# Sums kept in HBM, a gate applied in the last block, seven raw buffers and sums of weights by adding transfers, in the MLP of a two-layer trunk

## The chip, the cores and the metric

The kernel runs on one core of a Trainium2 chip. The metric is the device time of one execution in microseconds (us); the median of three runs is 2183.13 us (2182.64 to 2187.89). Engines are named as in the profile: PE multiplies matrices, PEld loads its weights, DVE (vector), ACT (scalar) and POOL work on tiles, and SP only issues transfers.

## The reference

Two layers over 256 tokens of width 2048. Each has an attention part and an MLP, both modulated by vectors computed from a condition `c`. In short:

```python
cond = silu(c)
for l in range(2):
    mod = cond @ w_ada[l] + b_ada[l]                # 2048 x 12288
    sh_a, sc_a, g_a, sh_m, sc_m, g_m = split(mod, 6)
    h = rmsnorm(x) * (1 + sc_a) + sh_a
    mix = attention(h, w_in[l], ...)                 # two kinds of heads
    x = x + g_a * (mix @ w_o[l])
    h = rmsnorm(x) * (1 + sc_m) + sh_m
    y = square(relu(h @ w_mlp_in[l])) @ w_mlp_out[l] # 2048 -> 8192 -> 2048
    x = x + g_m * y
return rmsnorm(x, final_norm_g)
```

Everything is float32.

## The kernel before

**Weights.** Each float32 product is made of three: a weight of 128 rows by 2048 columns (1 MB) is loaded by SP into a buffer with the tag `raw`, ACT copies its high part `hi` (line 152, in halves of 1024 columns), DVE subtracts to get the low part `lo` (line 155), and PE multiplies high by high, high by low and low by high. There are five `raw` buffers and four each of `hi` and `lo`. Loads are issued in the order of SP's queue, and one waits until a buffer is free.

**Conditioning loads.** `w_ada` is 192 such loads of 1 MB. They use the same five buffers. They are not multiplied on PE: DVE multiplies each by `cond` and sums it in one instruction (line 381), writing to `macc`, and then makes columns of `mod`. When they are loaded is set by a rate: each call of `weights` adds `self.rate` to a credit, and for each whole unit one load is issued (`more_ada`). `RATE_S` is the rate in the paired part of a block, `RATE_R` in its second part, and the other `RATE_` names hold in other stages.

**The MLP.** Its 8192 hidden columns are cut into four blocks of 2048 (`fb` 0 to 3). A block first makes the hidden activations and then multiplies them with `w_mlp_out`. Layer 0's first block goes through `first_block`; all others go through `block_by_seven`, which works in pairs of 128 hidden columns: two `wides` (a weight each, 32 matmuls, to bank `ps`) make the pair's hidden tile; then `seven` multiplies it with the left 1024 output columns by seven products of 2x2 blocks in place of eight. The products go in two steps, `five` and `two`, into seven PSUM banks `pp`, which are summed over the pairs of the block. The weights of that step are one load (`raw<-in_w_ms`) and three sums of its parts, which DVE writes to a second `raw` buffer under the name `comb` (lines 1223 to 1225). Line 1223 is the largest, 128 x 1024. There are eight pairs in a block, five in the first block of layer 1, whose first three pairs are made another way (`plain`).

After the pairs comes the second part of the block, called its tail below: the right 1024 columns as two groups (`c` = 2 and 3), each with four weights (`in_w_m`) and 96 matmuls into two banks `pr`.

**What is kept.** The seven sums of a block are added to tiles `acc` in SBUF: by ACT's copy to `part` and a transfer of POOL that adds 256 KB (`acc<-part`, lines 1145 and 1146), or by DVE in the last block (line 1142). The right columns of each block are multiplied by the gate `self.row` (named `bias` in the profile; DVE, line 1151) and added to the residual `x` by a transfer of POOL (`x<-yg`, line 1154). The gate of a layer is computed in its second block.

**Order.** The program is written stage by stage, and a tile scheduler sets the order of instructions on each engine. Each engine and each queue runs in its order.

Of the kernel before, what the change touches and what calls it, by code (L numbers as in the profile page):

```python
# [97 lines left out]
RATE_A0, RATE_V, RATE_A1, RATE_A2, RATE_K, RATE_K1, RATE_M0, RATE_R = 1.1, 1.6, 0.7, 1.2, 0.6, 0.4, 1.0, 1.25  # L98
RATE_S = 0.0, 0.3
# [3 lines left out]
class Trunk:  # L103
    def __init__(self, ctx, tc, io):
# [4 lines left out]
        self.up = pool("up", 44)  # L109
        self.tp = pool("tp", 8)  # L110
# [58 lines left out]
    def raw(self, src, width):  # L169
        raw = self.wp.tile([P, width], F32, tag="raw", name=self.name("raw"), bufs=5)  # L170
        self.nc.sync.dma_start(raw, src)
        return raw
# [189 lines left out]
    def ada_load(self):  # L362
        w = self.wp.tile([P, D], F32, tag="raw", name=self.name("ada"), bufs=5)
# [519 lines left out]
    def layer(self, l, acc=None):  # L883
# [164 lines left out]
        acc, late = ({}, []) if l else self.first_block(h, banks)  # L1048
        for fb in range(1 - l, NFB):
            self.block_by_seven(l, fb, h, banks if l and fb == 0 else [], acc, late)  # L1050
        self.quiet = False

    def first_block(self, h, banks):

        io = self.io
        hid, acc, late = [], {}, []
# [3 lines left out]
        for m in range(12, NK, 2):  # L1060
            ps = self.wides([io["w_m10"][m + j - 12] for j in range(2)], h)
            hid += self.relu2(self.joined(ps, self.t("sum")))
        for c in range(4):
            pss = self.rows(io["w_m2"][0, 0], hid, c)
            if c == 0:
                acc[2], acc[4] = [self.copy(ps, "acc") for ps in pss]
            elif c == 1:
                acc[3], acc[7] = [self.copy(ps, "acc") for ps in pss]
                self.nc.vector.tensor_tensor(acc[4], acc[7], acc[4], ALU.subtract)
            else:  # L1070
                late += [(self.copy(ps, "y"), t, c) for t, ps in enumerate(pss)]
        return acc, late

    def block_by_seven(self, l, fb, h, banks, acc, late):

        io = self.io
        hid, steps, sums = [], [], []
        plain = len(banks)
        self.rate = RATE_S[l] if fb == 0 or not l else 0.0
        for m in range(0, plain, 2):  # L1080
            hid += self.relu2(self.joined(banks[m : m + 2], self.t("sum")))
        for m in range(plain, NK, 2):
            both = self.t("sum")
            for j in range(2):
# [3 lines left out]
                if m > plain + 2:  # L1088
                    steps.pop(0)()
# [3 lines left out]
            steps += self.seven(io[f"w_ms{l}"][fb, m // 2], parts, r, sums, m == plain, m == NK - 2)  # L1093
            if fb == 1 and m == 2:
                self.gate(l, 5)
            while m > 4 and late:
                self.add_late(*late.pop(0))
        for f in steps:
            f()
        self.rate = RATE_R  # L1100
        end = fb == NFB - 1
        light = [lambda g=g: self.gather(acc, sums, g, end) for g in ((1, 2), (3, 5), (7, 6), (4,))]
        halves = []
        if end:
            done = self.final if l else lambda pss, c: self.updates(pss, c, True)
            light += [lambda: halves.extend(self.merged(acc))]
            light += [lambda c=c: done(halves[c], c) for c in range(2)]
        elif fb:
            def done(pss, c):
                for t in range(2):  # L1110
                    self.add_late(pss[t], t, c)
        else:
            def done(pss, c):
                late.extend((self.copy(ps, "y"), t, c) for t, ps in enumerate(pss))
        light.pop(0)()
        pss = [self.bank("pr") for _ in range(2)]
        for kq in range(4):
            self.rows_by_k(pss, self.weights(io["w_m2"][l, fb, 2, kq]), hid, kq)
            if light:
                light.pop(0)()  # L1120
# [3 lines left out]
        if plain:  # L1124
            self.both_by_k([self.weights(io[f"w_ms{l}"][fb, m // 2]) for m in range(0, plain, 2)], hid, acc)
        if end:
            pss = self.rows(io["w_m2"][l, fb], hid, 3, True)
        else:
            pss = [self.bank("pr") for _ in range(2)]
            for kq in range(4):  # L1130
                self.rows_by_k(pss, self.weights(io["w_m2"][l, fb, 3, kq]), hid, kq)
        done(pss, 3)

    def gather(self, acc, sums, group, end):

        flat = lambda v: v.rearrange("p a b -> p (a b)")
        for i in group:
            ps = sums[i - 1]
            if i not in acc:
                acc[i] = self.copy(ps, "acc")  # L1140
            elif end:
                self.nc.vector.tensor_tensor(acc[i], ps, acc[i], ALU.add)
            else:
                t = self.t("part")
                self.nc.scalar.activation(t, ps, AF.Copy)
                self.nc.gpsimd.dma_start(flat(acc[i]), flat(t), accum_op=ALU.add)

    def add_late(self, y, t, c):

        tmp = self.t("yg").rearrange("p a b -> p (a b)")  # L1150
        self.nc.vector.tensor_tensor(
            tmp, y.rearrange("p a b -> p (a b)"), self.row[:, 512 * c : 512 * c + 512], ALU.mult
        )
        self.nc.gpsimd.dma_start(self.xs_of(t, c), tmp, accum_op=ALU.add)
# [521 lines left out]
```

## Time and profile before

| | |
|---|---|
| median of the runs | 2183.13 us |
| the profiled execution | 2184.29 us, of which 2182.5 us are the span of the profile |
| PE busy | 2125.5 us, 97% |
| DVE busy | 1868.8 us, 86% |
| ACT busy | 1268.2 us, 58% |
| POOL busy | 49.7 us, 2% |
| transfers issued by SP, share of 16 DMA engines | 586.41 MB, 72.0% |
| transfers issued by POOL | 18.12 MB, 3.9% |

Busy shares are means over stages, so each stage is to be read by itself. A row of a group of instructions gives line, engine, operation, written and read tiles, count, then busy time and mean duration in ns, then the engine's idle time ahead of it and what ended that. A row of a transfer gives its issuer, count, size and the median time in us from issue to landing. `x` in a row of the windows is a count of instructions. Some matmuls are missing in the records, and a busy PE is not always at its peak.

### The profile page before, as it was taken

How to read it: one execution, taken by the hardware profiler on the slowest of the kernel's cores; microseconds unless marked ns; L12 is line 12 of the kernel's file. 1: busy time of each engine (PE TensorE's matmuls, PEld its weight loads, DVE VectorE, ACT ScalarE, POOL GpSimd, SP SyncE). 2: the span in 40 equal slices, each digit the busy share in tenths (PEclk: the TensorE clock that was granted, in tenths of full speed). 3: DMA queues.
4: the chain of work that ended last, by engine and by line, in shares of the span. 5: the costliest groups of instructions: out<-in, count | busy, mean ns of one | idle time of the engine just before them, and what ended most of it. 6: DMA issues, size and time to landing. Idle time of an engine off the chain costs nothing.

```text
span 2182.5 us, 29752 instructions
## 1 busy us (share of the span) xinstructions
PE 2125.5 (97%) x11339; PEld 1828.8 (84%) x11339; DVE 1868.8 (86%) x2558; ACT 1268.2 (58%) x1872; POOL 49.7 (2%) x67
## 2 busy tenths in 40 slices
PE   7999999999999899899989999999999999999998
PEld 6899887998888788788869998878878888888886
DVE  8889888888899798788998898789997985895898
ACT  6555663554467366456555566536655674774674
POOL 0000000000000000100000000000000010000000
PEclk8999999999999999999999999999999999999999
DMA  9989899789965965976679779896696767468453
GB/s 397 422 335 347 318 360 345 275 313 373 366 211 203 371 230 190 299 280 220 224 262 338 273 289 337 312 347 247 212 344 253 234 226 230 174 219 257 178 195 130
DMA packets 94304, 607.64 MB, mean 278 GB/s; under 512 B 10640, under 2 KB 11088, under 8 KB 27344
## 3 DMA queue, kind: packets, MB, share of 16 engines
q1 hardware_dynamic: 85536, 586.41, 72.0%
q0 software_dynamic: 7904, 18.12, 3.9%
q8 instruction: 89, 1.46, 0.2%
q10 hardware_dynamic: 720, 1.19, 0.1%
q14 instruction: 55, 0.45, 0.1%
HBM read 589.66 MB, written 3.18 MB: 272 GB/s over the span
## 4 chain that ended last, share of the span: by engine, by line
PE 81%; DVE 9%; DMA 6%; ACT 2%; issue 1%; ACTq 0%; DVEq 0%
PE ps L218 18%; PE ps L221 10%; PE pr L312 6%; PE pr L313 6%; PE pr L315 6%; DVE lo L155 4%; DMA raw<-in_w_m 3%; PE pk L261 3%; PE pp L1216 3%; PE pp L1215 3%; PE pp L1214 3%; DVE ada L381 2%; PE pk L195 2%; PE pk L199 2%; PE pk L198 2%; PE pk L285 2%
## 5 line engine op out<-in xcount | busy, mean ns | idle before, releaser
L152 ACT ACTIVATE hi<-raw 128x1024 fp32r<-128x1024 f32 (+2 forms) x714 | 706.1, 1004 | 552.9 <-DMA raw<-in_w_m 143.2
L155 DVE TENSOR_TENSOR lo<-raw,hi 128x1024 fp32r<-128x1024 f32 (+2 forms) x714 | 808.3, 1153 | 211.8 <-ACT hi L152 131.5
L381 DVE SCALAR_TENSOR_TENSOR ada<-ada,cond 128x2048 f32<-128x2048 f32 x192 | 437.2, 2284 | 13.5 <-DMA ada<-in_w_ada 12.8
L218 PE MATMUL ps<-h,hi 128*128 128x512 f32 x1856 | 442.6, 391 | 0.4 <-DVE sum L1382 0.3
L218 PEld LDWEIGHTS ps<-h,hi 128*128 128x128 f32 x1856 | 344.4, 188 | 75.0 <-DVE sum L1382 5.0
L312 PE MATMUL pr<-hi,hidh 128*128 128x512 f32 x576 | 229.4, 398 | 17.5 <-ACT hi L152 17.3
L221 PEld LDWEIGHTS ps<-h,lo 128*128 128x128 f32 x1856 | 237.4, 191 | 8.7
L221 PE MATMUL ps<-h,lo 128*128 128x256 f32 x1856 | 240.1, 283 | 0.0
L313 PE MATMUL pr<-hi,hidl 128*128 128x512 f32 x576 | 227.2, 395 | 0.0
L312 PEld LDWEIGHTS pr<-hi,hidh 128*128 128x128 f32 x576 | 110.0, 191 | 47.8 <-ACT hi L152 25.0
L315 PE MATMUL pr<-lo,hidh 128*128 128x512 f32 x576 | 144.7, 392 | 5.4 <-DVE lo L155 5.4
L155 DVE TENSOR_TENSOR lo<-comb,hi 128x1024 fp32r<-128x1024 f32 x106 | 128.9, 1218 | 7.7 <-PE ps L221 7.2
L315 PEld LDWEIGHTS pr<-lo,hidh 128*128 128x128 f32 x576 | 108.4, 189 | 29.5 <-DVE lo L155 7.1
L313 PEld LDWEIGHTS pr<-hi,hidl 128*128 128x128 f32 x576 | 110.1, 191 | 22.8
L152 ACT ACTIVATE hi<-comb 128x1024 fp32r<-128x1024 f32 x106 | 111.4, 1054 | 24.5 <-PE pp L1216 14.7
L195 PE MATMUL pk<-h,hi 128*128 128x256 f32 x320 | 90.4, 285 | 0.2 <-ACT h L716 0.2
L199 PE MATMUL pk<-h,lo 128*128 128x256 f32 x320 | 90.5, 283 | 0.0
L198 PE MATMUL pk<-h,hi 128*128 128x256 f32 x320 | 90.5, 283 | 0.0
L1381 ACT ACTIVATE sum<-ps 128x256 f32<-128x256 f32 x110 | 42.2, 383 | 80.5 <-PE ps L221 80.5
L261 PE MATMUL pk<-hf,w 128*128 128x256 f32 x384 | 83.9, 379 | 0.0
L1215 PE MATMUL pp<-lo,sh 128*128 128x512 f32 x212 | 83.4, 393 | 0.2 <-DVE lo L155 0.2
L1214 PE MATMUL pp<-hi,sh 128*128 128x512 f32 x212 | 81.9, 394 | 1.0 <-ACT sh L1205 1.0
(295 smaller groups left out, 3521.3 us busy)
## 6 DMA issues: line engine op xcount, KB each, us to landing
ada<-in_w_ada SPq DMA_DIRECT2D x192, 1024.0 KB, 6.9
raw<-in_w_m SPq DMA_DIRECT2D x182, 1024.0 KB, 6.3
raw<-in_w_ms SPq DMA_DIRECT2D x56, 1024.0 KB, 5.2
raw<-in_w_o SPq DMA_DIRECT2D x32, 1024.0 KB, 6.5
raw<-in_w_m SPq DMA_DIRECT2D x24, 768.0 KB, 5.9
raw<-in_w_dv SPq DMA_DIRECT2D x16, 1024.0 KB, 6.1
raw<-in_w_t SPq DMA_DIRECT2D x12, 1024.0 KB, 6.6
w<-in_w_a SPq DMA_DIRECT2D x24, 384.0 KB, 13.5
```

The costliest lines, as they stand in the source:

```text
L152: ins = self.nc.scalar.activation(hi, v, AF.Copy)
L155: ins = self.nc.vector.tensor_tensor(lo, v, hi.bitcast(F32), ALU.subtract)
L198: mm(ps, hi, x[1], start=False, stop=False, skip_group_check=shared)
L218: mm(ps.rearrange("p a b -> p (a b)"), part(w, k, 0), x[2], start=k == 0, stop=False)
L221: mm(ps[:, 0], part(w, k, 1), x[0], start=False, stop=k == nk - 1)
L261: self.nc.tensor.matmul(ps, v, whole[k], start=first, stop=last, skip_group_check=True)
L312: mm(ps, xh[:, c], part(i, 0), start=kq == 0 and i == 0, stop=False)
L313: mm(ps, xl[:, c], part(i, 0), start=False, stop=False)
L315: self.last_mm = mm(ps, xh[:, c], part(i, 1), start=False, stop=kq == 3 and i == 3)
L381: ins = nc.vector.scalar_tensor_tensor(w, w, 1.0, self.cond, ALU.mult, ALU.mult, accum_out=acc[:, i : i + 1])
L1214: nc.tensor.matmul(ps, x[0], wh, start=first, stop=False)
L1215: nc.tensor.matmul(ps, x[0], wl, start=False, stop=False)
```

## The change

It has five parts.

- The seven sums of a block and its right columns are kept in tiles `kept` in HBM. ACT copies each bank to `part`, and a transfer of POOL writes it (the first time) or adds it there (`keep`, `keep_tile`, `keep_left`, `keep_right`). In the last block, `last_right` has POOL load the eleven kept tiles of 256 KB into SBUF, and DVE adds the last sums to them.
- The gate is computed and applied in the last block only: `rows(2)` and `rows(3)` multiply the kept right columns by it, and POOL adds them to `x`.
- Seven buffers `raw` in place of five; the pool `up` (2 KB per partition) goes from 44 to 40, `tp` from 8 to 6, and the scratch for POOL's transfers from 4096 to 2048.
- The largest sum of weights is made by ACT (a copy with scale -1) and a transfer of POOL that adds 512 KB to it, one pair ahead of its use (`sums_of_weights`); DVE still makes it for the last pair of a block. That is 46 by transfer and 7 by DVE, where DVE made 53.
- The rates: conditioning loads are fewer in the tails (`RATE_R`, `RATE_E`) and some are now in the paired part of all blocks of layer 0.

Over the program POOL's rows go from 72 to 168, DVE's from 2274 to 2206, ACT's from 1674 to 1738; PE's and SP's stay at 10616 and 595.

```diff
-RATE_A0, RATE_V, RATE_A1, RATE_A2, RATE_K, RATE_K1, RATE_M0, RATE_R = 1.1, 1.6, 0.7, 1.2, 0.6, 0.4, 1.0, 1.25
-RATE_S = 0.0, 0.3
+RATE_A0, RATE_V, RATE_A1, RATE_A2, RATE_K, RATE_K1, RATE_M0 = 1.1, 1.6, 0.6, 1.1, 0.6, 0.4, 0.9
+RATE_S, RATE_R, RATE_E = (0.45, 0.25), (0.6, 0.4), 0.5
+RAWS = 7
...
-        self.rate = RATE_S[l] if fb == 0 or not l else 0.0
+        self.rate = RATE_S[l]
...
-                if m > plain + 2:
-                    steps.pop(0)()
+                if j == 0 and pairs:
+                    pairs[-1][0]()
+                if len(pairs) > 1:
+                    pairs[-2][1 + j]()
...
+        self.rate = RATE_E if end else RATE_R[l]
         if end:
...
+            return self.last_right(l, hid, sums)
+        light = [lambda g=g: [self.keep(i, sums[i - 1]) for i in g] for g in ((1, 2), (3, 5), (7, 6), (4,))]
         light.pop(0)()
+        for c in (2, 3):
+            pss = [self.bank("pr") for _ in range(2)]
+            for kq in range(4):
+                self.rows_by_k(pss, self.weights(io["w_m2"][l, fb, c, kq]), hid, kq)
+                if light:
+                    light.pop(0)()
+            self.keep_right(pss, c)
...
+    def last_right(self, l, hid, sums):
...
+        def loads():
+            for i in list(range(1, 8)) + [(t, c) for c in (2, 3) for t in range(2)]:
+                acc[i] = self.u("acc")
+                self.nc.gpsimd.dma_start(acc[i].rearrange("p a b -> p (a b)"), self.kept[i])
...
+        def rows(c):
+            for t in range(2):
+                y = acc[t, c].rearrange("p a b -> p (a b)")
+                op(y, y, self.row[:, 512 * c : 512 * c + 512], ALU.mult)
+                self.nc.gpsimd.dma_start(self.xs_of(t, c), y, accum_op=ALU.add)
...
+    def keep_tile(self, i, t):
+        t = t.rearrange("p a b -> p (a b)")
+        if i in self.kept:
+            self.nc.gpsimd.dma_start(self.kept[i], t, accum_op=ALU.add)
         else:
...
+            self.kept[i] = self.dp.tile([P, 2 * T], F32, name=f"kept{self.n}")
+            self.nc.gpsimd.dma_start(self.kept[i], t)
...
+        def sums_of_weights(by_dve=False):
+            raw = self.raw(src, 2048)
+            comb = self.wp.tile([P, 2048], F32, tag="raw", name=self.name("comb"), bufs=RAWS)
+            if by_dve:
+                add(comb[:, :1024], raw[:, 512:1536], raw[:, :1024], ALU.subtract)
+            else:
+                nc.scalar.activation(comb[:, :1024], raw[:, :1024], AF.Copy, scale=-1.0)
+                nc.gpsimd.dma_start(comb[:, :1024], raw[:, 512:1536], accum_op=ALU.add)
+            st["raw"], st["comb"] = raw, comb
...
         def five():
+            raw, comb = st["raw"], st["comb"]
             if first:
                 sums.extend(self.bank("pp") for _ in range(7))
-            raw = self.raw(src, 2048)
-            comb = self.wp.tile([P, 2048], F32, tag="raw", name=self.name("comb"), bufs=5)
-            add(comb[:, :1024], raw[:, 512:1536], raw[:, :1024], ALU.subtract)
             add(comb[:, 1024:1536], raw[:, 1024:1536], comb[:, :512], ALU.subtract)
```

How it moves instructions. First SP's queue, in the tail of the third block of layer 0; `in_w_m` are weights of the right columns, `in_w_ada` conditioning loads. Before:

```order
L171 DMA raw_8153<-in_w_m 128x2048
L365 DMA ada_8166<-in_w_ada 128x2048
L171 DMA raw_8198<-in_w_m 128x2048
L365 DMA ada_8209<-in_w_ada 128x2048
L171 DMA raw_8238<-in_w_m 128x2048
L365 DMA ada_8250<-in_w_ada 128x2048
L171 DMA raw_8284<-in_w_m 128x2048
L365 DMA ada_8295<-in_w_ada 128x2048
L365 DMA ada_8297<-in_w_ada 128x2048
L171 DMA raw_8323<-in_w_m 128x2048
```

The same place now:

```order
L172 DMA raw_8236<-in_w_m 128x2048
L172 DMA raw_8274<-in_w_m 128x2048
L366 DMA ada_8284<-in_w_ada 128x2048
L172 DMA raw_8318<-in_w_m 128x2048
L366 DMA ada_8330<-in_w_ada 128x2048
L172 DMA raw_8356<-in_w_m 128x2048
L172 DMA raw_8391<-in_w_m 128x2048
L366 DMA ada_8401<-in_w_ada 128x2048
L172 DMA raw_8427<-in_w_m 128x2048
L172 DMA raw_8471<-in_w_m 128x2048
```

Between five weights there were five conditioning loads; between seven there are now three.

Second DVE's row in the first pairs of layer 0's fourth block; `ps` are banks of the `wides`, `comb` the sums of weights (and, with 128 columns, those of the hidden tile). Before:

```order
L1206 TENSOR_TENSOR sl_8549<-comb_8543,sh_8548 128x512
L1224 TENSOR_TENSOR comb_8714<-raw_8712,comb_8714 128x512
L155 TENSOR_TENSOR lo_8719<-raw_8712,hi_8718 128x512
L1225 TENSOR_TENSOR comb_8714<-comb_8714,raw_8712 128x512
L155 TENSOR_TENSOR lo_8726<-raw_8712,hi_8725 128x1024
L1382 SCALAR_TENSOR_TENSOR sum_8552<-ps_8598,sum_8552 128x256
L1223 TENSOR_TENSOR comb_8864<-raw_8862 128x1024
```

The same place now:

```order
L382 SCALAR_TENSOR_TENSOR ada_8481,macc_88<-ada_8481,cond 128x2048
L156 TENSOR_TENSOR lo_8584<-raw_8581,hi_8583 128x1024
L156 TENSOR_TENSOR lo_8588<-raw_8581,hi_8587 128x1024
L1415 SCALAR_TENSOR_TENSOR sum_8469<-ps_8470,sum_8469 128x256
L1258 TENSOR_TENSOR comb_8629<-raw_8627,comb_8629 128x512
L1259 TENSOR_TENSOR comb_8629<-comb_8629,raw_8627 128x512
L156 TENSOR_TENSOR lo_8636<-raw_8633,hi_8635 128x1024
L156 TENSOR_TENSOR lo_8640<-raw_8633,hi_8639 128x1024
L1415 SCALAR_TENSOR_TENSOR sum_8469<-ps_8517,sum_8469 128x256
L382 SCALAR_TENSOR_TENSOR ada_8591,macc_88<-ada_8591,cond 128x2048
```

The 128x1024 sum is gone from the row, conditioning rows have come in, and the two remaining sums (lines 1258 and 1259, 1224 and 1225 before) stand further ahead of the low parts made from `comb`. They read what POOL's transfer has added.

Third, where the copy of that chain and those adds stand, in a pair in the middle of a block of layer 1. ACT's row now, `comb_17333` being the sum (before, ACT had no such row):

```order
L153 ACTIVATE hi_17204<-comb_17031 128x1024
L153 ACTIVATE hi_17217<-raw_17215 128x1024
L1231 ACTIVATE sh_17130<-comb_17125 128x512
L1250 ACTIVATE comb_17333<-raw_17331 128x1024
L1414 ACTIVATE sum_17134<-ps_17135 128x256
L153 ACTIVATE hi_17221<-raw_17215 128x1024
L153 ACTIVATE hi_17259<-comb_17031 128x1024
L153 ACTIVATE hi_17289<-raw_17287 128x1024
```

DVE's row now, over the same stretch:

```order
L156 TENSOR_TENSOR lo_17218<-raw_17215,hi_17217 128x1024
L1415 SCALAR_TENSOR_TENSOR sum_17134<-ps_17135,sum_17134 128x256
L156 TENSOR_TENSOR lo_17222<-raw_17215,hi_17221 128x1024
L156 TENSOR_TENSOR lo_17260<-comb_17031,hi_17259 128x1024
L156 TENSOR_TENSOR lo_17290<-raw_17287,hi_17289 128x1024
L1258 TENSOR_TENSOR comb_17333<-raw_17331,comb_17333 128x512
L1259 TENSOR_TENSOR comb_17333<-comb_17333,raw_17331 128x512
L156 TENSOR_TENSOR lo_17294<-raw_17287,hi_17293 128x1024
```

ACT's copy stands between the halves of one weight of a `wides` (`raw_17215`), and DVE's adds between the halves of the next (`raw_17287`).

More of the change, by code (lines that the diff above doesn't have):

```diff
@@ L1055, in first_block @@
         io = self.io
-        hid, acc, late = [], {}, []
+        hid = []
         self.rate = RATE_M0
@@ L1092, in block_by_seven @@
             hid += parts
-            steps += self.seven(io[f"w_ms{l}"][fb, m // 2], parts, r, sums, m == plain, m == NK - 2)
-            if fb == 1 and m == 2:
+            pairs.append(self.seven(io[f"w_ms{l}"][fb, m // 2], parts, r, sums, m == plain, m == NK - 2))
+            if end and m == 2:
                 self.gate(l, 5)
[L1096 to L1101, printed above, removed]
@@ L1167, in merged, with both_by_k @@
         return [a2, a4], [a3, a5]
-    def both_by_k(self, ws, xs, acc):
+    def both_by_k(self, ws, xs):
         mm = self.nc.tensor.matmul
         flat = lambda v: v.rearrange("p a b -> p (a b)")
-        pss = [[flat(self.bank("pr")) for _ in range(2)] for _ in range(2)]
+        banks = [[self.bank("pr") for _ in range(2)] for _ in range(2)]
         last = 2 * len(ws) - 1
```

130 lines of the change are left out of this document (61 added, 69 removed).

## The prediction

> **What bounds the kernel now.** I read the busy shares and queues first, then where the matrix engine (PE) is not full, then what it waits for there.
>
> ```profile
> span 2182.5 us, 29752 instructions
> PE 2125.5 (97%) x11339; PEld 1828.8 (84%) x11339; DVE 1868.8 (86%) x2558; ACT 1268.2 (58%) x1872; POOL 49.7 (2%) x67
> q1 hardware_dynamic: 85536, 586.41, 72.0%
> q0 software_dynamic: 7904, 18.12, 3.9%
> PE 81%; DVE 9%; DMA 6%; ACT 2%; issue 1%; ACTq 0%; DVEq 0%
> ```
>
> The last line is the chain that ended last: PE holds 81%, and 15% is DVE and DMA, so there are places where PE is fed late. A change that leaves the matmuls alone can only win those. They stand out when the same 192 matmuls, the right columns of a block (its "tail"), are compared block by block. The rows are the second to fourth block of layer 0, then those of layer 1; columns are window, its length, busy time and count of PE, weight loads, DVE, ACT, POOL, then granted clock, DMA share, GB/s.
>
> ```profile
> core 0: us, PE busy (x) PEld busy (x) DVE busy (x) ACT busy (x) POOL busy (x), PEclk, DMA share, GB/s
> 712.40:763.33 50.93, 44.47 (x192) 35.54 (x191) 39.29 (x41) 17.25 (x20) 4.37 (x5) 1.00 1.03 374
> 891.69:947.98 56.29, 48.29 (x194) 37.94 (x192) 39.17 (x40) 19.21 (x22) 6.22 (x7) 0.94 1.03 357
> 1077.35:1131.61 54.26, 48.08 (x193) 37.66 (x192) 51.55 (x65) 20.64 (x31) 0.00 (x0) 0.94 0.83 295
> 1786.97:1830.27 43.30, 43.30 (x193) 35.85 (x191) 21.92 (x21) 20.47 (x22) 6.17 (x7) 1.00 0.93 296
> 1958.59:2002.11 43.52, 43.52 (x194) 36.04 (x192) 21.85 (x20) 20.57 (x22) 6.19 (x7) 1.00 0.93 290
> 2130.49:2174.17 43.68, 43.68 (x193) 35.86 (x191) 38.33 (x52) 20.48 (x31) 0.00 (x0) 1.00 0.29 103
> ```
>
> Layer 1 does them in 43.5 us with PE never idle; layer 0 takes 7.4, 12.8 and 10.8 us more, 31 us together. In the first two the DMA engines are full (1.03); in the third DVE is (51.55 of 54.26). What layer 0 has there and layer 1 has not is the conditioning loads, `ada`: DVE time of that tile alone, two rows counted per load, so 9, 9, 7 and none:
>
> ```profile
> 712.40:763.33 50.93, 20.48 (x18) 1.00 1.03 374
> 891.69:947.98 56.29, 20.47 (x18) 0.94 1.03 357
> 1077.35:1131.61 54.26, 15.98 (x14) 0.94 0.83 295
> 1786.97:1830.27 43.30, 0.00 (x0) 1.00 0.93 296
> ```
>
> The chain of waits in the second of these tails is three waits for a weight, and ACT, which makes the high parts, sat 31.4 us behind it:
>
> ```profile
> 892.79 10.54 DMA raw<-in_w_m
> 906.98 11.64 DMA raw<-in_w_m
> 925.60 8.52 DMA raw<-in_w_m
> L152 ACT ACTIVATE hi<-raw 128x1024 fp32r<-128x1024 f32 x18 | 18.1, 1055 | 37.1 <-DMA raw<-in_w_m 31.4 <-PE pr L315 5.6
> ```
>
> The pairs of the `seven` stretches ahead of those tails are the opposite: five windows of one pair each (three of layer 0, two of layer 1) sum to a full PE, with DVE at 14 of 16 us and the DMA half idle. The other rows are the first block of layer 1 in its pairs, where DVE is at 96% and PE loses 1.4 us in 50, then four stretches with small losses: the last half of layer 0's first block, layer 1's `w_o`, the end of layer 1's first block, layer 0's `w_o`.
>
> ```profile
> 791.14:807.30 16.16, 16.16 (x88) 13.89 (x87) 14.38 (x23) 11.40 (x16) 0.00 (x0) 1.00 0.54 195
> sum 79.81, PE 79.81 PEld 68.53 DVE 69.94 ACT 55.48 POOL 0.00; mean PE 15.96 PEld 13.71 DVE 13.99 ACT 11.10 POOL 0.00
> 1542.00:1592.00 50.00, 48.59 (x252) 40.80 (x251) 48.13 (x66) 33.62 (x45) 0.00 (x0) 1.00 0.60 212
> 494.60:584.20 89.60, 88.81 (x387) 71.54 (x386) 75.92 (x76) 36.59 (x42) 0.00 (x0) 1.00 0.98 373
> 1393.50:1475.20 81.70, 78.72 (x344) 64.67 (x343) 71.23 (x83) 32.14 (x45) 0.00 (x0) 0.98 0.91 339
> 1597.75:1659.00 61.25, 59.78 (x262) 48.83 (x261) 50.79 (x52) 26.71 (x30) 0.00 (x0) 1.00 0.97 376
> 320.20:401.50 81.30, 79.08 (x358) 64.18 (x357) 70.32 (x83) 35.82 (x52) 0.00 (x0) 1.00 0.89 337
> ```
>
> **The change part by part.** Prices first: DVE's sum of weights and its conditioning row with the read-out (of nine in a tail), an add from a bank; then a 20 us window with four accumulating transfers of 256 KB and its queues, their landing, the late landings with seven transfers in a row in a tail of layer 1, POOL's time for an issue (least, median, most), and the usual landings of weights.
>
> ```profile
> L1223 DVE TENSOR_TENSOR comb<-raw 128x1024 f32<-128x1024 f32 x53 | 64.6, 1219 | 5.0 <-DMA raw<-in_w_ms 5.0
> L381 DVE SCALAR_TENSOR_TENSOR ada<-ada,cond 128x2048 f32<-128x2048 f32 x192 | 437.2, 2284 | 13.5 <-DMA ada<-in_w_ada 12.8
> L381 DVE DVE_READ_ACCUMULATOR ada<-ada,cond 128x1 f32 x9 | 0.7, 82 | 0.0
> L1142 DVE TENSOR_TENSOR acc<-pp,acc 128x512 f32<-128x512 f32 x5 | 3.3, 685 | 0.0
> q1 hardware_dynamic: 550, 4.00, 51.1%
> q0 software_dynamic: 576, 1.05, 30.1%
> x<-yg POOLq DMA_DIRECT2D x4, 256.0 KB, 4.3
> raw<-in_w_m SPq DMA_DIRECT2D x5, 1024.0 KB, 11.5
> acc<-part POOLq DMA_DIRECT2D x7, 256.0 KB, 13.6
> L1146 POOL DMA_DIRECT2D acc<-part x25: 860/872/1967, 710.2 to 1965.1; - x25
> raw<-in_w_m SPq DMA_DIRECT2D x182, 1024.0 KB, 6.3
> raw<-in_w_ms SPq DMA_DIRECT2D x56, 1024.0 KB, 5.2
> ```
>
> In that window 16 engines spent 51.1% of 20 us on 4.00 MB: 2.7 us for a load of 1 MB, 0.67 us for 256 KB. The four accumulates took 30.1%: 1.5 us each, 2.2 times a plain copy.
>
> *Rates: fewer conditioning loads in the tails.* Layer 0's tails go from 1.25 loads per weight to 0.6 (0.5 in the last): with eight weights, about 4.8, 4.8 and 4 in place of 9, 9 and 7. With the 11 accumulates of a block (seven kept sums, four right rows), DMA work of the second of the three tails was 8 x 2.7 + 9 x 2.7 + 11 x 1.5 = 62 us against 43.5 us of matmuls; it becomes 8 x 2.7 + 4.8 x 2.7 + 11 x 1.5 = 51. The 7 us left over must come from loads made ahead in the half-idle pairs, and each of the two buffers added (five to seven) holds one load of 2.7 us, so 5.4 of 7 are covered. I take 44 us for the first tail (three of its 11 kept sums are plain copies at 0.67, so 48.6 of DMA work), 44.5 for the second, 46.5 for the third, where DVE's 51.55 us lose 3 loads of 2.3 and gain four multiplications of 0.69 (about 47.5 us, not all inside the window). Gain 6.9 + 11.8 + 7.8 = **26.5 us** of the 31; its bounds are 14 (nothing covered: 48.6, 51 and 47.5 us, so 2.3, 5.3 and 6.8) and 31.
>
> *The same in the other stretches.* Rate 1.25 to 0.6 in the last half of layer 0's first block, 384 matmuls, 87.0 us at 43.5 per 192, measured 89.6: I take 1.5 of 2.6. End of layer 1's first block, 61.25 with PE busy 59.78, rate to 0.4: 1.2 of 1.5. The pairs of layer 1's first block: rate 0.3 to 0.25 and no sum on DVE, so 48.13 us in 50 less three sums of 1.22 is 89%, near the 88% of the pairs that lose nothing: 1.4 in 50 over five pairs of 16 us is 2.2, I take 1.9. The two `w_o` stretches lose 3.0 and 2.2 us of PE on late weights; seven buffers and rates lowered by 0.1 ahead of them: 2.5 and 1.3. Together **8.4**, bounds 0 and 11.
>
> *Where those loads go.* Into the pairs of layer 0: 0.45 per weight is 0.9 per pair. DVE there: 13.99 less 1.22 for the sum that leaves it, plus 0.9 x 2.37 (the load's row and its 0.08 read-out): 14.9 of 15.96, 93%. Rows on either side: 88% with no loss, 96% with 1.4 in 50. Between them by proportion 1.9%, over 24 pairs (383 us) 7.2: I take **-7**, bounds 0 and -11 (the 96% row). Cover is gone if DVE passes 100%; then weights' low parts are late.
>
> *Sum of weights by ACT, POOL and a transfer*, for 46 of 53. DVE loses 46 x 1.22 = 56 us, counted above. ACT gains a copy of 1.06 per pair on 11.1 of 15.96: hidden. POOL issues 46 more, 0.86 to 1.97 each, on a nearly idle engine. The DMA work of a pair is three loads of 2.7, 0.9 of `ada` and an accumulate of 512 KB at 3.0, or 13.5 of 15.96 us, with 54% before. What matters is lateness: two DVE adds wait in order for the transfer, and every low part stands behind them. From the start of the copy the chain is 1.06 for the copy, then issue to landing: 256 KB take 4.3 in a quiet stretch and 1.5 more for double the bytes make 5.8; a load met on the way adds up to 2.7, and in a queue like the tail's it is 13.6 or more. So 7 to 10 us, 15 at worst. The room is read from the rows: in about half of the pairs the adds stand one `wides` behind the copy, in the others one and a half to two. A matmul of 512 columns takes 43.5/192 = 0.227, the 21 of the seven products of a pair 4.8, so a `wides` is (15.96 - 4.8)/2 = 5.6 us. DVE then waits 1.4 to 4 us in half of the pairs. In layer 1 it has room for that, 13.99 - 1.22 = 12.8 of 15.96, and low parts are made a few us ahead; in layer 0, with 14.9 of 15.96, some of it reaches PE. I take 1 us in one pair of four there (6 of 24), a little of it hidden: **-5**, bounds 0 and -24 (1 us in each). The weight and its sum also stay longer in their buffers, which uses up the two buffers added while pairs run; in a tail they are free again for loads.
>
> One rule of the Trainium skill speaks against it ("SBUF — State Buffer", section "SBUF: two separate sides"): while DVE runs certain two-port operations GpSimd is shut out of their shared port and can't write descriptors, and a transfer of some 620 ns took some 3100. By it each chain would be 2.5 us longer, an estimate from that page, and a wait of 4 to 6.5 us in half of the pairs. The trace shows no such lock: issues take 0.86 us in the median in tails where DVE is 70 to 77% busy. The same skill fits such a transfer as 2.0 us plus bytes at 436 GB/s ("DMA: Bandwidth & Descriptors", section on the SWDGE path), 3.2 us for 512 KB, an estimate that ignores the accumulation; the trace's 4.3 us for 256 KB is already above it.
>
> *Kept sums in HBM.* POOL's accumulates of 256 KB go from 49 to 55, beside 44 plain copies and loads. No row shows an accumulate whose target is in HBM; the nearest is 1.5 us into SBUF, a plain copy 0.67 is the floor, double, 3.0, a ceiling. I take 1.5. Over the run: 46 x 3.0 + 55 x 1.5 + 44 x 0.67 - 49 x 1.5 = 176 us, so the share goes from 76% to 84%; nothing waits for these but the last blocks' 11 loads, and they are read a block later. DVE loses 24 multiplications by the gate and gains 8 in the last tails; the banks `pr` and `pp` are emptied by ACT copies, and ACT is under half busy in every tail. The last tails hold 11 loads of 0.67 in place of nothing, with the DMA at 0.29 in layer 1. After layer 1's last matmul come the same steps as before; four multiplications more and waits for loads: **-0.7** (bounds 0 and -3). The gate moves to the last blocks, when the conditioning sums it needs have long been loaded: 0. The smaller pools (`up` 40, `tp` 6, half the scratch for POOL's transfers) cost 0 as long as the transfers that empty them land within a tail, as 13.6 us does; if not, ACT's copies wait, and behind them the high parts.
>
> Sum: 26.5 + 8.4 - 7 - 5 - 0.7 = 22.2. The profiled execution took 2184.3 us (span 2182.5 and 1.8 around it) and the median is 1.2 less, so 2184.3 - 22.2 = 2162.1 there and **2161 us** as a median. Its bounds: 14 + 0 - 11 - 24 - 3 = -24 (2207) if every term fails together, 31 + 11 = 42 (2141) if all go well.
>
> **Rivals.** *Sums come late (slower).* If the transfer lands as in the tail, 13.6 us after its issue, the chain is 14.7 us against 5.6 to 11 of room. DVE stands 4 to 9 us, lags ACT by what the four low-part buffers allow, and the rest stops PE. From 0.6 us per pair (46 x 0.6 = 28) all that is left of the gain (22 + 5) is gone; at 1.5 us it is 69, 2161 + 69 - 5 = 2225. For it: POOL's queue is in order, 13.6 is a measured landing, and the wait stands ahead of all low parts. Against: that was seven transfers in a row beside weights landing in 11.5; in pairs there is one, the DMA was 54% busy, weights land in 5.2 to 6.3. 10%.
>
> *Tails stay bound by DMA.* If an accumulate into HBM costs 3.0 us, the two first of layer 0's tails and the two middle ones of layer 1 get 12 to 16 us more DMA work; layer 1's were at 0.93 already. With the added buffers as cover I price it at 6 us for each of four: 24 us back, 2185. Against: the bytes moved are the same as into SBUF. 8%.
>
> *The stall only moves into layer 0's pairs.* If `ada` in a pair makes DVE pass its limit, -11 to -20 in place of -7: 2165 to 2174. For it: the row at 96%. 15%, still faster.
>
> *More than forecast*: the buffers cover everything, 2141 to 2150, no wait for sums among it. 12%.
>
> **How the numbers follow.** My case, 2151 to 2169, has 55%. With the third and fourth rival 82% lie in 2141 to 2174; the range 2144 to 2178 leaves out the late sums, the dear accumulates and a little at the low end, 2 in 10. About 0.3%, 6.5 us, is what a measurement can tell. Faster 0.82: my case and the last two. Same 0.08: dear accumulates. Slower 0.10: late sums.
>
> **What would show it.** Right: layer 0's three tails at 43.5 to 47 us for 192 matmuls; no wait of ACT for weights over 2 us there; DVE some 93% in layer 0's pairs with PE at 98%; landing of the `comb` transfer at 6 to 9 us, and DVE idle for it under 3 us a time. Wrong: DVE idle behind that transfer by more, with PE idle behind DVE's low parts; `kept` transfers over 2 us of all engines each; tails at DMA share 1.0 with 50 us; pairs over 16.5 us.

## The result: slower by 2.3%

| | before | changed |
|---|---|---|
| median | 2184.76 us | 2235.64 us |
| ratio, with its 95% interval | | 1.0233 (1.0215 to 1.0251) |
| span of the profiled execution | 2182.5 us | 2232.4 us |

The forecast was 2161 us, faster. It went the way of the first rival, the late sums (2225). From the page of the changed kernel:

```profile
span 2232.4 us, 30091 instructions
PE 2141.9 (96%) x11339; PEld 1835.7 (82%) x11339; DVE 1803.0 (81%) x2490; ACT 1315.7 (59%) x1938; POOL 119.3 (5%) x163
q1 hardware_dynamic: 85536, 586.41, 69.6%
q0 software_dynamic: 18912, 55.36, 11.2%
```

DVE has 66 us less to do than before and yet the span is 50 us longer. ACT and POOL have more to do (48 and 70 us), but they are busy for 59% and 5% of the span. PE is busy 16 us longer with the same number of matmuls, so some of them took longer; the rest of the 50 us is PE standing idle. The windows of the tails (layer 0's second to fourth block, then layer 1's; columns as in the prediction):

```profile
core 0: us, PE busy (x) PEld busy (x) DVE busy (x) ACT busy (x) POOL busy (x), PEclk, DMA share, GB/s
729.95:773.47 43.52, 43.52 (x193) 36.05 (x192) 32.08 (x32) 21.89 (x26) 5.59 (x8) 1.00 1.02 374
927.42:970.95 43.53, 43.53 (x193) 36.05 (x192) 31.97 (x32) 21.87 (x26) 6.55 (x8) 1.00 1.04 348
1124.20:1169.33 45.13, 44.25 (x193) 35.76 (x192) 44.93 (x61) 19.54 (x28) 3.54 (x4) 1.00 0.89 311
2180.35:2224.04 43.69, 43.69 (x193) 35.86 (x191) 40.56 (x58) 20.29 (x31) 3.54 (x4) 1.00 0.35 111
```

The three tails that took 50.9, 56.3 and 54.3 us take 43.5, 43.5 and 45.1: 29.3 us won, with PE never idle in two of them. The loss is ahead of them. The stretch from the end of one tail to the start of the next, for layer 0's second to fourth block and layer 1's first to third; first before, then changed:

```profile
584.20:712.40 128.20, 128.12 (x683) 110.07 (x682) 116.59 (x161) 89.79 (x120) 5.51 (x7) 1.00 0.64 226
763.33:891.69 128.36, 128.26 (x681) 109.71 (x680) 116.41 (x159) 88.23 (x117) 3.56 (x4) 1.00 0.60 214
947.98:1077.35 129.37, 128.78 (x681) 109.62 (x680) 116.34 (x160) 84.85 (x111) 1.77 (x2) 1.00 0.59 208
...
1659.00:1786.97 127.97, 127.97 (x683) 109.99 (x682) 112.26 (x156) 87.25 (x117) 6.36 (x8) 1.00 0.60 208
```

```profile
579.60:729.95 150.35, 136.11 (x681) 113.52 (x680) 117.98 (x162) 94.88 (x124) 8.58 (x11) 0.95 0.72 240
773.47:927.42 153.95, 136.95 (x681) 113.17 (x680) 117.36 (x162) 92.22 (x122) 9.30 (x11) 0.94 0.74 238
970.95:1124.20 153.25, 137.89 (x682) 113.37 (x681) 117.44 (x162) 91.80 (x121) 14.92 (x22) 0.94 0.77 260
1506.80:1638.30 131.50, 123.20 (x655) 102.95 (x653) 111.70 (x168) 87.97 (x133) 4.66 (x6) 0.99 0.69 233
1698.14:1835.27 137.13, 130.62 (x681) 109.06 (x680) 111.84 (x155) 90.81 (x121) 7.70 (x10) 1.00 0.73 242
1878.83:2008.95 130.12, 128.35 (x681) 109.63 (x680) 103.05 (x144) 89.71 (x121) 8.30 (x10) 1.00 0.69 229
```

Layer 0's stretches lose 22, 26 and 24 us, and those of layer 1's first three blocks 8, 9 and 2 (123.15 before in its first, 128.32 in its third). Of the 72 us of layer 0, 46 are PE idle. The other 26 are PE busy for longer on the same matmuls: 136.1, 137.0 and 137.9 us in place of 128.1, 128.3 and 128.8, at a granted clock of 0.95, 0.94 and 0.94 in place of 1.00. The waits of layer 0's third block (engine, tile and line, what it waited for: us in total, times, longest) name the cause:

```profile
ACT relu L1422 <- DVE sum L1415: 18.1, 7, 9.6
DVE comb L1258 <- DMA comb<-raw: 17.9, 5, 6.9
PEld pp L1241 <- DVE lo L156: 17.1, 8, 6.2
ACT sh L1231 <- DVE comb L1229: 15.0, 5, 7.5
PE pp L1241 <- DVE lo L156: 13.4, 7, 5.7
```

DVE stands for the adding transfer (second line). Behind it in DVE's row are low parts and pieces of the hidden tile, so ACT waits for DVE (first and fourth line), and PE for DVE's low parts. Two windows one behind the other in the same block show what that does to PE:

```profile
802.11:822.36 20.25, 15.37 (x57) 11.38 (x55) 16.11 (x22) 10.56 (x15) 0.86 (x1) 0.75 0.68 219
822.36:846.27 23.91, 18.18 (x87) 15.16 (x87) 15.05 (x21) 12.05 (x16) 0.87 (x1) 0.86 0.57 153
```

The second is a whole pair, 23.9 us in place of 16; the first holds one `wides` of the two. PE stands idle for 4.9 and 5.7 us in them, and the granted clock is 0.75 and 0.86. In the three pairs that follow it is 1.00, with PE idle for 2.9 us or less in each. So a wait costs PE twice here, while it stands and in the slower matmuls around it. That the standing brings the clock down is read from such rows; no run changed the clock by itself. Over the run DVE's wait for the transfer is 91 us, ahead of its instruction of line 1258:

```profile
L1258 DVE TENSOR_TENSOR comb<-raw,comb 128x512 f32<-128x512 f32 x53 | 36.5, 689 | 97.1 <-DMA comb<-raw 91.1
DMA to landing us min/median/max: 4.4/6.2/14.7
```

The second line is the flight of the 46 transfers. They come in two kinds. One of layer 0's third block, 821.4 to 832.4 us, and one of layer 1's last, 2097.7 to 2102.4, with the queues in just that time:

```profile
q1 hardware_dynamic: 356, 2.57, 73.0%
q0 software_dynamic: 144, 0.52, 24.1%
...
comb<-raw POOLq DMA_DIRECT2D x1, 512.0 KB, 11.0
```

```profile
q0 software_dynamic: 144, 0.52, 61.1%
q1 hardware_dynamic: 17, 0.14, 15.3%
...
comb<-raw POOLq DMA_DIRECT2D x1, 512.0 KB, 4.7
```

The engines spend nearly the same on it, 0.241 x 11.0 = 2.65 and 0.611 x 4.7 = 2.87 us. In the first case SP's loads moved 2.57 MB beside it, in the second 0.14.

### The profile page after: what moved, and what is told of

It reads as the page before. It is cut to its first block, busy times and chain, and to the rows that moved or that the text cites. A ratio compares the mean times of both kernels' runs of the same rounds, so it can differ in the third digit from the quotient of the medians.

```text
span 2232.4 us, 30091 instructions
## 1 busy us (share of the span) xinstructions
PE 2141.9 (96%) x11339; PEld 1835.7 (82%) x11339; DVE 1803.0 (81%) x2490; ACT 1315.7 (59%) x1938; POOL 119.3 (5%) x163
## 5 line engine op out<-in xcount | busy, mean ns | idle before, releaser
L219 PE MATMUL ps<-h,hi 128*128 128x512 f32 x1856 | 450.9, 396 | 8.7 <-DVE sum L1415 5.1
L219 PEld LDWEIGHTS ps<-h,hi 128*128 128x128 f32 x1856 | 350.0, 191 | 90.1 <-DVE sum L1415 10.2
L313 PE MATMUL pr<-hi,hidh 128*128 128x512 f32 x576 | 224.1, 389 | 0.0
L156 DVE TENSOR_TENSOR lo<-comb,hi 128x1024 fp32r<-128x1024 f32 x106 | 129.3, 1220 | 12.6 <-PE ps L222 7.6
L1258 DVE TENSOR_TENSOR comb<-raw,comb 128x512 f32<-128x512 f32 x53 | 36.5, 689 | 97.1 <-DMA comb<-raw 91.1
L1422 ACT ACTIVATE relu<-sum 128x512 f32<-128x512 f32 x58 | 36.5, 629 | 80.6 <-DVE sum L1415 80.5
```

The lines of the kernel that those rows point to most:

```text
L156: ins = self.nc.vector.tensor_tensor(lo, v, hi.bitcast(F32), ALU.subtract)
L219: mm(ps.rearrange("p a b -> p (a b)"), part(w, k, 0), x[2], start=k == 0, stop=False)
L313: mm(ps, xh[:, c], part(i, 0), start=kq == 0 and i == 0, stop=False)
```

## The experiments

Ratios are to the kernel before, timed on the same chip, with 95% intervals.

**1. DVE makes all sums (`dve_sums`).**

```diff
-            if by_dve:
+            if True:
                 add(comb[:, :1024], raw[:, 512:1536], raw[:, :1024], ALU.subtract)
```

> The changed kernel (2236 us) with one part undone: DVE makes all 53 large sums of weights again, still one pair ahead; rates, seven buffers and kept sums stay as changed. Theory 'late sums' (DVE stands for the adding transfer, and with it the chain of the hidden tile): the 72 us that layer 0's pairs lost go down to some 10 and the 19 of layer 1 to 5 or less, so 2236 - 76 = 2160 us, between 2153 and 2172. Rival 'conditioning rows overload DVE': DVE's work in a pair of layer 0 rises from 14.9 to 16.1 us of 15.96, so the pairs stay as slow or get slower, above 2210 us.

2156.09 us, ratio 0.9862 (0.9844 to 0.9881). This one part cost 80 us, and the rest of the change is worth some 30. It is the best version found, and beats both kernels. The busy times of its page, and layer 0's stretches:

```profile
PE 2113.6 (98%) x11339; PEld 1824.0 (85%) x11339; DVE 1851.5 (86%) x2536; ACT 1279.6 (59%) x1892; POOL 78.8 (4%) x117
579.53:718.05 138.52, 132.71 (x684) 111.22 (x683) 125.45 (x169) 87.35 (x119) 3.00 (x5) 0.99 0.64 233
760.89:893.27 132.38, 129.76 (x684) 110.08 (x683) 124.29 (x169) 87.59 (x117) 4.10 (x6) 1.00 0.71 252
936.11:1068.61 132.50, 129.88 (x686) 110.18 (x684) 124.23 (x170) 86.61 (x114) 8.70 (x15) 1.00 0.75 277
```

DVE has 7 us more work per block here than in the changed kernel (124.29 against 117.36), and the blocks are 12 to 22 us shorter. The rival that DVE is overloaded by conditioning rows falls; the three stretches still take some 16 us more than before (17.5 by the windows, of which 2 are three matmuls of the tail that stand inside each window here). PE is busy for 2113.6 us in place of 2141.9, with a granted clock of 0.998 over the run in place of 0.985. So of the 78 us between the two spans, 50 were PE standing idle and 28 slower matmuls.

**2. The rates as before, transfers kept (`old_rates`).**

```diff
-RATE_S, RATE_R, RATE_E = (0.45, 0.25), (0.6, 0.4), 0.5
+RATE_S, RATE_R, RATE_E = (0.0, 0.3), (1.25, 1.25), 1.25
```

> The changed kernel with the rates of the pairs and tails as before (0 and 0.3 in the pairs, 1.25 in all tails); the sums of weights stay with the adding transfer. Theory 'late sums, because SP's loads crowd the transfer': without conditioning loads in layer 0's pairs the transfer lands in 4.5 to 6 us as in layer 1's later blocks, the pairs lose some 5 us a block in place of 24, and the tails give part of it back (10 to 20 us): about 2190 us, between 2180 and 2205. Rival 'the transfer is late by itself': still 9 to 11 us to landing in layer 0's pairs, pairs as slow, 2235 to 2260 us.

2235.56 us, ratio 1.0221 (1.0198 to 1.0244): a miss. The time is that of the rival, but the rival's ground, 9 to 11 us to landing, holds only for the first transfers of a block. In the trace the later transfers of a block land in 4.6 us even in layer 0, with pairs of 16 us and PE full:

```profile
819.00:835.00 16.00, 16.00 (x86) 13.67 (x85) 12.85 (x18) 12.04 (x16) 0.87 (x1) 1.00 0.67 230
DMA to landing us min/median/max: 4.4/4.7/11.2
```

But the first two or three of each block of layer 0, which follow a tail full of loads, still take 8 to 11 us, so layer 0's stretches are 138.8, 137.6 and 146.4; the tails went back to 46.8, 50.0 and 56.2, and layer 1's first block got 14 us longer, with 22 conditioning loads in it in place of 11. Beside conditioning loads the transfer lands later, but they are not all that delays it.

**3. The adds written later (`late_adds`).**

```diff
         def two():
+            add(comb[:, 1024:1536], raw[:, 1024:1536], comb[:, :512], ALU.subtract)
+            add(comb[:, 1536:], comb[:, 1024:1536], raw[:, 1536:], ALU.subtract)
             w = self.part(st["comb"], 1, 1024)[0]
```

(and the same two lines taken out of `five`)

> The changed kernel with DVE's two small adds, which wait for the transfer, moved from the step of five products to the step of two, where their result is first used. The transfer itself is as late as before. Theory 'DVE stands in order for the transfer': the first use is then the low part of the sum in the step of five, several us later in DVE's row, so the wait shrinks: 30 to 60 us back, 2175 to 2205 us. Rival 'DVE is short of time in layer 0's pairs': no row is taken from it, so 2230 us or more.

2238.65 us, ratio 1.0234 (1.0207 to 1.0261). Neither theory is tested by it: the wait is where it was.

```profile
DVE comb L1269 <- DMA comb<-raw: 93.8, 28, 10.5
```

The adds stand at the same place in DVE's row as before: the scheduler put them there although they are written later in the program.

**4. The new rates alone, on the kernel before (`new_rates`).** The three lines of the diff that set rates.

> The kernel before with the changed rates alone: five buffers, sums of weights by DVE, sums kept in SBUF. DVE's work in a pair of layer 0 is then 13.99 + 2.1 = 16.1 of 15.96 us. Theory 'late sums': only a little is lost in the pairs (10 to 15 us), the tails gain 20 to 25: 2165 to 2178 us. Rival 'conditioning rows overload DVE': the pairs of layer 0 lose 40 us or more, 2195 us or more.

2171.73 us, ratio 0.9935 (0.9913 to 0.9958), some 15 us faster, inside what 'late sums' expected. Conditioning rows in layer 0's pairs do not overload DVE as the rival said.

**5. The adds tied back in DVE's row (`adds_behind`).**

```diff
+            w, low = self.part(comb, 0, 1024)
+            ins = add(comb[:, 1024:1536], raw[:, 1024:1536], comb[:, :512], ALU.subtract)
+            self.behind(ins, low)
+            add(comb[:, 1536:], comb[:, 1024:1536], raw[:, 1536:], ALU.subtract)
```

> The changed kernel (2236 us), transfers as they are, with the first of DVE's two small adds tied behind the low part of the sum (in the run before this the adds stayed at their place in DVE's row, 94 us of waiting, since the scheduler puts them where it takes them to be ready). DVE then first meets the transfer at that low part, some 20 rows later than now. Theory 'DVE stands in order for the transfer': the transfer has about 10 us more and is there in most pairs; 50 to 80 us back, 2155 to 2185 us. Rival 'the transfer is late for its true use as well': ACT and DVE stand at the parts of the sum itself, above 2210 us.

2184.87 us, ratio 1.0005 (0.9994 to 1.0015): 51 of the 80 us come back, with the time at the upper end of what was expected, from transfers that land no earlier:

```profile
DMA to landing us min/median/max: 4.5/10.5/11.9
ACT hi L153 <- DVE comb L1266: 65.7, 40, 3.7
DVE lo L156 <- issue: 87.0, 40, 3.6
```

No engine waits for the transfer any more in this trace, so most of the cost was the place of the wait in DVE's row. What is left looks like the adds now being close to their use: ACT waits 66 us for them. That this is the 29 us was not tested.

**6. The transfer in layer 1 alone (`transfer_l1`).**

```diff
-            if by_dve:
+            if by_dve or not self.late_layer:
...
         self.rate = RATE_S[l]
+        self.late_layer = l == 1
```

> The changed kernel with the adding transfer in layer 1 alone (25 of 46); DVE makes the sums of layer 0. Against all sums by DVE (2156 us) only layer 1's loss should come back, which was 11.0, 9.3 and 2.2 us in its first three blocks by the stages of the traces: 2156 + 22 = 2178, between 2170 and 2185. Rival 'the cost is per transfer, whatever else is moved': 25/46 of 80 us, 2200.

2181.11 us, ratio 0.9989 (0.9980 to 0.9998): 25 to 28 us over all sums by DVE, for 25 of 46 transfers, as expected from layer 1's blocks and short of 25/46 of 80, or 43. So a transfer costs more in layer 0 than in layer 1. In layer 0 there are more loads beside it, and DVE has less time to spare in a pair; this run does not tell the two apart. Layer 1's last block costs nothing here either (128.1 us).

**7. Five buffers (`dve_five_raws`): experiment 1 with `RAWS = 5`.**

> All sums by DVE (2156 us with seven buffers), with five raw buffers. If the buffers carry the tails' gain, as in the forecast (two loads of 2.7 us each tail, and the stages with small losses), 15 to 30 us come back: 2171 to 2186. If the rates and the kept sums carry it, within 6 us: 2150 to 2162.

2254.56 us, ratio 1.0335 (1.0314 to 1.0357), far beyond both expectations. A weight and its sum held a pair longer leave three of five buffers for everything else, and ACT stands for weights, 181 us in place of 36 in experiment 1:

```profile
ACT hi L153 <- DMA raw<-in_w_m: 181.3, 64, 7.8
```

It shows that sums a pair ahead need the seven buffers, not what these are worth in the tails. For that there are the next two.

**8. Sums by DVE in their own pair (`dve_own_pair`).**

```diff
-        return [sums_of_weights, five, two]
+        return [lambda *a: None, lambda: (sums_of_weights(), five()), two]
```

> All sums by DVE, and made in their own pair as before, so that two buffers are held a pair shorter. If the early sums cost loads their room, layer 0's pairs (10 + 4 + 4 us lost) get faster: 2146 to 2154. If those pairs are bound by DVE at 16 of 16 us, no change: 2154 to 2158.

2161.67 us, ratio 0.9906 (0.9889 to 0.9922): against the expectation, a little slower than 0.9862. Made a pair ahead, DVE's sums are not in the way; the buffers held cost less than that.

**9. The same with five buffers (`own_pair_five_raws`).**

> All sums by DVE in their own pair (2162 us with seven buffers) with five raw buffers. With sums held a pair longer five buffers cost 98 us; here they are not. If the two added buffers are worth the 5 us of the tails that the forecast gave them and a little elsewhere, it comes near the new rates alone (2172 us, which differ from it by the kept sums): 2166 to 2178. If only the rates matter: 2160 to 2164.

2169.23 us, ratio 0.9929 (0.9913 to 0.9946). Two buffers are worth some 5 to 8 us. From the new rates alone (0.9935) it differs only by the kept sums, the gate and the smaller pools, so these together are worth nothing that can be told.

**10. Sums by DVE, seven buffers, old rates (`dve_old_rates`).**

> All sums by DVE a pair ahead, seven buffers, kept sums (2156 us), with the rates of the pairs and tails as before. The tails of layer 0 take 47, 50 and 56 us again and the first block of layer 1 some 6 more, as in the run with the old rates and transfers; the pairs lose nothing: 2156 + 4 + 7 + 11 + 11 - 15 = 2174, between 2165 and 2182. If the buffers alone had freed the tails: below 2156.

2172.43 us, ratio 0.9946 (0.9932 to 0.9961), as expected: beside experiment 1, the rates are worth 16 to 18 us. Layer 0's stretches are 127.5, 128.2 and 128.5 and its tails 47.1, 49.8 and 53.3. Experiment 2 is this kernel with the transfers: at these rates they cost some 60 us.

**11. Other rates (`dve_rates2`).** Experiment 1 with `RATE_A1`, `RATE_A2`, `RATE_M0` as before, 0.35 in layer 0's pairs, 0.7 and 0.6 in its tails.

> All sums by DVE (2156 us), with 0.35 in place of 0.45 in layer 0's pairs, 0.7 and 0.6 in the tails, and the earlier stages' rates as before the change. DVE's work in a pair goes from 16.0 to 15.6 of 15.96 us. If DVE binds those pairs, half of their 18 us comes back: 2145 to 2153. If not, 2154 to 2160.

2160.91 us, ratio 0.9890 (0.9876 to 0.9905): a miss. The third and fourth blocks, tails included, won 1.4 and 0.7 us, but the second lost 2.5 and the attention of layer 1, with the higher rates, 3.9. DVE is not what binds the second block's pairs alone; what does was not followed.

**12. The sum made by POOL (`pool_sums`).**

```diff
-                nc.scalar.activation(comb[:, :1024], raw[:, :1024], AF.Copy, scale=-1.0)
-                nc.gpsimd.dma_start(comb[:, :1024], raw[:, 512:1536], accum_op=ALU.add)
+                nc.gpsimd.tensor_tensor(comb[:, :1024], raw[:, 512:1536], raw[:, :1024], ALU.subtract)
```

> The changed kernel with the large sum made by POOL itself in one operation, in place of ACT's copy and the adding transfer. No run has shown POOL's time for it. If it takes a few us and slows nobody, DVE is relieved and nothing waits for a transfer: 2135 to 2152 us. If it takes over 8 us, or DVE's operations beside it get longer, the sums come late again: above 2165.

2225.06 us, ratio 1.0190 (1.0170 to 1.0211). As the second case had it, DVE's operations beside POOL's get longer. From the groups of layer 0's third block:

```profile
L156 DVE TENSOR_TENSOR lo<-raw,hi 128x1024 fp32r<-128x1024 f32 x27 | 39.1, 1463 | 0.0
...
L1250 POOL TENSOR_TENSOR comb<-raw 128x1024 f32<-128x1024 f32 x5 | 17.1, 3422 | 76.7 <-DVE lo L156 76.7
```

In this block DVE does not wait for the sum, but over the run it stands 49.8 us for POOL's result, in 12 waits of up to 11.6 us. Which of the two costs more was not tested.

**13. Transfers that nobody reads (`transfers_unread`).** Beside experiment 1:

```diff
+                    nc.gpsimd.dma_start(self.kept["spare"], raw[:, 512:1536], accum_op=ALU.add)
```

> All sums by DVE (2156 us), and beside them 46 adding transfers of the same 512 KB from the same weights into a spare tile in HBM, which nothing reads: the traffic without the wait (and without ACT's copy; the sum's result does not depend on it). If what cost 80 us was waiting for the transfer, the traffic alone is nearly free: 2156 to 2168 us. If it was the traffic (loads of weights landing later, weights' buffers held by the transfer), most of the 80 us comes: above 2200.

2156.32 us, ratio 0.9875 (0.9860 to 0.9890), the same as experiment 1. The traffic, 24 MB through POOL's queue into HBM, is free, though the flights are as long:

```profile
span 2154.6 us, 30005 instructions
spare<-raw POOLq DMA_DIRECT2D x46, 512.0 KB, 7.1
```

So the cost is not in moving that much data. ACT's 46 copies of 1.06 us are not in this run either; whether any of the 80 us is theirs was not tested.

**14. Half the transfer (`half_transfer`).**

```diff
+                nc.scalar.activation(comb[:, :512], raw[:, :512], AF.Copy, scale=-1.0)
+                nc.gpsimd.dma_start(comb[:, :512], raw[:, 512:1024], accum_op=ALU.add)
+                add(comb[:, 512:1024], raw[:, 1024:1536], raw[:, 512:1024], ALU.subtract)
```

> The changed kernel with the first 512 of the 1024 columns of the large sum made by ACT and an adding transfer of 256 KB, the rest by DVE. If the wait is for the flight of the transfer, it lands some 3 to 5 us earlier in layer 0's pairs (5 to 7 us) and DVE, with 0.6 us more work in a pair, waits half as much: 2185 to 2210 us. If the lateness is that of the chain's start (the weight's load), little is won: 2220 to 2240.

2249.50 us, ratio 1.0306 (1.0281 to 1.0332), slower than both expected. The flight did shrink (in layer 0 from a median of 9.4 to 6.8 us by the single transfers of the two traces), but the waits did not:

```profile
DVE comb L1259 <- DMA comb<-raw: 108.8, 23, 8.9
DMA to landing us min/median/max: 3.2/5.8/14.2
```

In layer 0 DVE came to the adds 7.3 us after the start of ACT's copy with the whole transfer, and 4.4 with the half (medians of 21). With a shorter transfer DVE comes to the adds earlier, and the wait stays. So this run could not tell the flight from the start of the chain; that split stays open.

## Why the prediction was wrong

- **What bounds the kernel** was right: the tails, by conditioning loads. The term of 26.5 us measured 29.3 (7.4 + 12.8 + 9.1). Two tails ran at 43.5 although the DMA engines were at 1.02 and 1.04, which fits loads made ahead into the added buffers.
- **The other stretches**, 8.4: the end of layer 0's first block 2.5 (forecast 1.5), `w_o` 4.9 and 1.4 (2.5 and 1.3), the end of layer 1's first block 1.4 (1.2), its pairs 2.7 with sums by DVE (1.9). That is 12.9 in all, the excess mostly in one `w_o`.
- **Conditioning loads into layer 0's pairs**, -7: with sums by DVE those stretches are some 16 us over before, 2.3 times the term, though there DVE also has the sum. DVE's work in a pair was forecast at 14.9 us and is that, in a pair of 18.3 (layer 0's third block, changed kernel):

```profile
866.37:884.66 18.29, 16.51 (x87) 13.55 (x86) 14.90 (x22) 11.85 (x16) 0.87 (x1) 1.00 0.82 265
```

- **The sums, -5**: this step failed. Against the same kernel with DVE's sums it measured -80. Its parts were near: the transfer's own time 3.0 us forecast, 2.65 and 2.87 measured; chain 7 to 10, measured 10.7 in layer 0 from the copy's start; room 5.6 to 11, measured 3.5 to 10; waits of 1.4 to 4 us in half of the pairs, measured 91 us over 29 waits, or 3.1 each. What failed is the step from DVE's wait to PE. The working let 1 us in one pair of four of layer 0 through, and its bound of 24 let 1 us through in each. In fact PE stood 50 us more than with DVE's sums. The wait stands ahead of the low parts and of the hidden tile's pieces, and DVE has 1 us to spare in a pair of layer 0.
- **The clock** was put at nothing: the working takes 0.227 us for a matmul throughout. The other 28 of the 78 us are PE busy for longer at a lower granted clock. The prediction's own rows had the sign of it: in the two slowest tails before, PE was busy for 48.3 and 48.1 us at a clock of 0.94, with the same matmuls that take 43.5 at 1.00.
- **Layer 1** was said to have room for the wait. It lost 22 us against sums by DVE in its first three blocks, and none in the last, where transfers land in 4.4 to 6.6 us.
- **Kept sums in HBM** were priced rightly: in 30 us of a tail of layer 1 (2010 to 2040) POOL's queue moved 2.42 MB in 44.5% of the time, 5.5 us per MB, or 1.45 us for 256 KB where 1.5 was taken; the end after layer 1's last tail is no longer than before (8.4 and 8.3 us).

```profile
q0 software_dynamic: 1310, 2.42, 44.5%
```

- **The first rival** gave the direction, and nearly the time, the time by luck. Its 1.5 us per transfer was an assumed price (measured is 80/46 = 1.7), and its condition did not come: it had the transfer land 13.6 us after its issue and DVE stand 4 to 9 us. The median landing was 6.2 us, in layer 0 9.4, one of 46 took longer than 13.6, and DVE stood 3.1 us a time. What it had right is that the wait stands ahead of all low parts. It was given one chance in ten because the landing was taken to be short; short waits were enough.
- The rule of the Trainium skill on DVE shutting GpSimd out ("SBUF — State Buffer", section "SBUF: two separate sides") did not show in the transfers: POOL's issues stayed at 0.86 to 1.07 us, and unread transfers cost nothing. (The 0.86 us that the prediction calls the median is the least of its row; the median is 0.87.) In the run with the sum on POOL, where both engines read SBUF, each is slower: the low part takes 1463 ns in the mean in place of 1220, and POOL's operation 2.4 to 4.5 us. The same section of the Trainium skill says that a GpSimd operation that reads SBUF and a DVE operation with two inputs in SBUF shut each other out of the shared ports; the trace agrees.

## What to carry to other kernels

Work taken off a busy engine and given to a chain of copy, issue and transfer can cost that engine a wait at the place where it takes the result, and an engine that runs in order then holds back everything behind it. Price such a chain by the landing under load, not at rest, count the spare time of the waiting engine in each pair, and look at the granted clock wherever PE will stand: here that was a third of the loss. A trace shows where in the row the wait stands; moving it back gave 51 of the 80 us. Moving conditioning loads from a stretch with full DMA engines to one with half-idle ones was worth some 16 us, and two more buffers some 5; the adding transfers, at 80 us, undid both.

## What was not expected of the hardware

- An adding transfer of 512 KB within SBUF occupied the DMA engines for 2.65 and 2.87 us in the two flights shown, but landed after 11.0 us with 2.57 MB of loads moved beside it and after 4.7 with 0.14 MB.
- 24 MB of adding transfers beside a kernel whose two queues already took 78% of the DMA engines' time changed its time by nothing (2156.32 against 2156.09 us).
- The granted clock was 0.985 over the changed kernel and 0.998 with the sums on DVE, one core and the same matmuls: 28 us of PE's busy time. It was 0.75 in 20 us in which PE stood for 4.9.
- A subtraction of 128 x 1024 in float32 takes POOL 2.4 to 4.5 us, and stretches DVE's two-input operations beside it from 1.2 to up to 3.4 us each.

```profile
L156 DVE TENSOR_TENSOR lo<-raw,hi x714: 676/1218/3436, 111.7 to 2212.8; 128x1024 fp32r<-128x1024 f32 x134, 128x512 fp32r<-128x512 f32 x27, 128x768 fp32r<-128x768 f32 x18
```

Columns are least, median and most in ns, with the sum on POOL; the most was 1228 in the changed kernel.
